# A streaming encoder layer on one core: the first part's stores on ScalarE's and GpSimd's queues, v loads asked for later, a buffer for the bias constant, and transposes held back

## The chip, the cores and the metric

The kernel runs on one core of a Trainium2 chip. It has a matrix engine (TensorE, PE in the profile), a vector engine (VectorE, DVE), a scalar engine (ScalarE, ACT), a general engine (GpSimd, POOL) and a queue engine that only issues transfers (SyncE, SP). Each engine works off its own instructions in their order and waits on semaphores for the others. Transfers between the on-chip memory and HBM are issued from SP, ACT or POOL and are carried out by 16 DMA engines. The metric is the device time of one execution in microseconds.

## What is computed

One layer of an encoder over 2048 prompt rows and 64 sample rows of width 1024. A conditioned norm is followed by one combined projection; its columns go to a gated convolution of width 31 (with layer norm and swish), to attention over the own chunk of 64 rows and the eight chunks before it (with a norm of q and k and a learned bias by distance), and to two gates. The two mixers are merged and projected; then comes a conditioned norm and a gated feed-forward network.

```
h = rms_norm(x, norm1_g) * (1 + sc1) + sh1
z = h @ w_in
glu_a, glu_b, q, k, v, g_conv, g_attn = split(z)
u = glu_a * sigmoid(glu_b)
conv_out, conv_state = conv_module(u, conv_hist, ...)
q = rms_norm(q, q_norm_g); k = rms_norm(k, k_norm_g)
o = attend(q, k, v)            # band of 9 chunks, softmax
merged = sigmoid(g_conv) * conv_out + sigmoid(g_attn) * (o @ w_attn_out)
x = x + gt1 * (merged @ w_o)
h2 = rms_norm(x, norm2_g) * (1 + sc2) + sh2
gate, up = split(h2 @ w_ffn_in)
x = x + gt2 * ((silu(gate) * up) @ w_ffn_out)
```

The outputs are the new rows of both sequences, the last 30 rows of the convolution's input, and the k and v rows that are kept (the last 512 of the prompt, the 64 of the sample).

## The kernel before

**Precision.** Every fp32 product is three products of rounded halves: an operand is split into a high part (`hi`, a copy by ACT in the rounded type) and a low part (`lo`, source minus high, by DVE or POOL), and `mm3` adds high x high, high x low and low x high. So each intermediate that goes to HBM for a later product goes as two stores, `hi` and `lo`.

**Two parts.** The first part works through four blocks of about 512 rows (`PBLOCKS`) in the order of `ORDER`: for each block q, a quarter of the convolution's input, k, another quarter, v, two more quarters, then the 16 column groups of the gates. It leaves q, k, v, the attention output, the convolution output and the gates in HBM (`q_d`, `k_d`, `v_d`, `o_d`, `c_d`, `g_d`). The second part (`CBLOCKS`) merges, projects and runs the feed-forward network from there.

**How work is interleaved.** The Python code keeps a planner, `Stream`, with an estimated load per engine in ns. `stream.at(t, f)` puts off `f` until the planner's TensorE time has passed `t`; `stream.when("dve")` is the time by which DVE is expected to have done what it was given; generators in lanes (`work` for q and k rows, `attn`, `conv`, `tail`, `norm_lane`) yield the time from which they may go on. `PE_LAG` is 400 ns. The lane `work` holds at most three rows; starting a fourth pushes the oldest on. The framework below assigns buffers and semaphores and may issue an instruction ahead of ones written earlier when its operands and its buffer are free: the bias rows are written after the second quarter of the convolution, yet their first operation runs at 65.15 us.

**Weights.** `Weights.split` (L294) loads or splits a weight tile into `whi` and `wlo` (five buffers each). For keys used again (`in` and `qkv` in the first part, `fi` and `fo` in the second), `then` (L332) stores both halves on SP at L336, and later blocks load them at L313. For `in` and `qkv` the low half is made by DVE.

**Rows of q and k.** `qk_rows` (L825) squares and copies the row's PSUM bank on ACT, reduces on DVE, takes the inverse root on POOL (`r`), scales on DVE (`kn`), and after `PE_LAG` goes to `store_kq` (L794): four transposes on PE, `hi` on ACT, `lo` on DVE into a pair of buffers (`parts`, two of each), and two stores on SP (L810). Kept k rows go out at L844.

**Rows of v.** `store_v` (L814) writes a tile `vst`, of which there is one buffer; it is stored on SP at L821. Kept v rows go out at L854.

**Convolution states.** `convolve` (L1008) transposes 30 columns of `u` on PE as soon as it starts (first and last block) and stores them at L1017. `conv_norm` stores its halves at L1079, `finish_head` those of the attention at L1178.

**Attention.** `attend(i)` (L1216 on) fetches the head's q, k and v, computes scores and softmax, and then the product with v. `load_v` (L1151 on, transfers at L1154 and L1156) uses the tag `vv` with two buffers; the v of head i+1 is asked for at the beginning of head i, when its buffer is still that of head i-1.

**Bias.** `bias_rows` (L774) writes a table of 128 shifted copies of the bias by one 3 MB transfer on ACT's queue (L784, called the skew transfer), and then two copies of a constant from the tile `far` (L788) into the same table. `far` comes from the seven buffers of `temp`.

Of the kernel before, what the change touches and what calls it, by code (L numbers as in the profile page):

```python
# [16 lines left out]
P = 128  # L17
# [24 lines left out]
PL_LESS = 9e9  # L42
TT_LESS = 9e9
PE_LAG = 400.0
ON_ACT = (3,)
ON_POOL = ()
DMA_LAG = 4000.0
# [167 lines left out]
class Weights:  # L215
# [78 lines left out]
    def split(self):  # L294
        i = len(self.ready)
        key = self.keys[i]
        if key[0] == "mod":
            (src,), a, b = self.source(key)
            w = self.pool.tile([P, a, b], F32, tag="whi", name="wmod", bufs=self.held)
            self.sync.dma_start(w, src)  # L300
            self.ready.append((w, None))
            return
        its = self.need.get(i, ())
        if i in self.first:
            shape = [P, 4 * len(key) - 4, P]
        else:
            shape = list(self.loaded[its[0]].shape) if its else self.stored[key][1]
        hi = self.pool.tile(shape, F32R, tag="whi", name="whi", bufs=self.held)
        lo = self.pool.tile(shape, F32R, tag="wlo", name="wlo", bufs=self.held)
        self.ready.append((hi, lo))  # L310
        if not its:
            for t, d in zip((hi, lo), self.stored[key][0]):
                self.sync.dma_start(t.bitcast(F32), d)  # L313
            return
        e, name = (self.dve, "dve") if key[0] in ("in", "qkv", "fi") or key[0] == "wo" and key[1] % 2 else (self.gps, "pool")
        if i in self.first:
            parts = [(slice(4 * j, 4 * j + 4), self.operand(f, op)) for j, (f, op) in enumerate(key[1:])]
            self.stream.after("act", "pool")
        else:
            parts = [(slice(0, shape[1]), self.loaded[its[0]])]  # L320
        for c, src in parts:
            self.act.activation(hi[:, c], src, AF.Copy)
            self.stream.after(name, "act")
            e.tensor_tensor(lo[:, c], src, hi[:, c].bitcast(F32), ALU.subtract)
        n = 0
        for j in its:
            self.users[j] -= 1
            if not self.users[j]:
                self.loaded.pop(j)
                n = j + 1 + self.staging  # L330

        def then():  # L332
            if key in self.again and key not in self.stored:
                ds = [self.dram.tile(shape, F32, name="w_d" + "_".join(map(str, key)) + "_" + part) for part in "hl"]
                for t, d in zip((hi, lo), ds):
                    self.sync.dma_start(d, t.bitcast(F32))  # L336
                self.stored[key] = ds, shape
            self.load_to(n)

        self.stream.at(self.stream.when(name), then, True)  # L340
# [87 lines left out]
def streaming_layer(ctx: ExitStack, tc: tile.TileContext, I, O):  # L428
# [147 lines left out]
    def temp(name, shape=(P, 512)):  # L576
        return wk.tile(list(shape), F32, tag="t", name=name, bufs=NT)

    def parts(n=None, shape=(P, 512)):
        return (  # L580
            wk.tile(list(shape), F32R, tag="sh", name="part_h", bufs=NS),
            wk.tile(list(shape), F32R, tag="sl", name="part_l", bufs=NS),
        )
# [103 lines left out]
    def mod_steps():  # L687
        for c6, half in MOD_HALVES:
            pa = ps_g.tile([P, 512], F32, tag="gp", name="pa")
            mod_sums(pa[:, : 2 * P], [("mod", c6, half, i) for i in range(4)])  # L690
            R = mod_rows(pa[:, : 2 * P])
            stream.at(
                stream.when("dve"), lambda pa=pa, R=R, c6=c6, half=half: mod_columns(pa[:, 2 * P :], R, c6, 4 * half, 2)
            )
            yield
        stream.flush()
        pt = ps_g.tile([P, 512], F32, tag="gp", name="pt")
        pe.transpose(pt[:32, :P], gates_c.rearrange("p c s k -> p (c s k)"), ident)
# [75 lines left out]
    def bias_rows():  # L774
        rv = wk.tile([NH, 257], F32, tag="bias", name="rv", bufs=1)
        nc.scalar.dma_start(rv, I["rel_bias"].rearrange("l h r -> (l h) r"))
        rr = wk.tile([NH, 768], F32, tag="kk", name="rr", bufs=1)
        dve.memset(rr[:, :511], 0.0)
        dve.tensor_scalar(rr[:, :511], rr[:, :511], rv[:, 256:], 8.0, ALU.add, ALU.mult)
        dve.tensor_scalar(rr[:, 511:], rv[:, ::-1], 8.0, None, ALU.mult)  # L780
        nc.scalar.dma_start(rb_d, rr)

        skew = bass.AP(tensor=sk_d.tensor, offset=sk_d.offset, ap=[[(P + 1) * 768, NH], [769, P], [1, 768]])
        nc.scalar.dma_start(skew, rb_d.unsqueeze(1).to_broadcast([NH, P, 768]))  # L784
        far = temp("far")
        dve.memset(far, BIG)
        for r, c in ((0, 576), (HD, 0)):
            nc.scalar.dma_start(  # L788
                sk_d[:, r : r + HD, P - 1 + c : P - 1 + c + HD].rearrange("h q c -> q h c"),
                far[:HD].rearrange("p (h c) -> p h c", h=NH),  # L790
            )


    def store_kq(src, n, dst, col, g=None):  # L794

        pt = ps_g.tile([P, 4, P], F32, tag="gp", name="pt")
        for hp in range(4):
            pe.transpose(pt[:, hp, :n], src[:n, hp * P : (hp + 1) * P], ident[:n, :n])
        stream.after("act", "pe")
        hi, lo = parts(shape=(P, 4, P))  # L800
        if g is None:
            split(hi[:, :, :n], lo[:, :, :n], pt[:, :, :n])
        else:
            act.activation(hi[:, :, :n], pt[:, :, :n], AF.Copy, scale=g)
            stream.after("dve", "act")
            dve.scalar_tensor_tensor(lo[:, :, :n], pt[:, :, :n], g, hi[:, :, :n].bitcast(F32), ALU.mult, ALU.subtract)

        def store():
            for j, t in enumerate((hi, lo)):
                nc.sync.dma_start(dst[j, :, :, col : col + n].rearrange("h p t -> p h t"), t[:, :, :n].bitcast(F32))  # L810

        stream.at(stream.when("act", "dve"), store)

    def store_v(src, n, row):  # L814
        vst = wa.tile([P, 4, 4, HD], F32R, tag="vst", name="vst", bufs=1)
# [5 lines left out]
        stream.at(stream.when("act", "dve"), lambda: nc.sync.dma_start(  # L821
            v_d[row : row + n].rearrange("t h d -> t (h d)"), vst[:n].rearrange("p a c d -> p (a c d)").bitcast(F32)
        ))

    def qk_rows(ps, n, g, dst, col, out_rows):  # L825
# [14 lines left out]
        if out_rows is not None:  # L840
            ko = temp("ko", (P, NH, HD))
            e, name = either(512, TT_LESS)
            e.tensor_tensor(ko[:n], kn[:n], gk[:n].unsqueeze(1).to_broadcast([n, NH, HD]), ALU.mult)
            stream.at(stream.when(name), lambda: nc.sync.dma_start(out_rows, ko[:n].rearrange("p h d -> p (h d)")))  # L844
        yield t + PE_LAG
        store_kq(kn.rearrange("p h d -> p (h d)"), n, dst, col, g)

    def v_rows(ps, n, t):
        out = state_row(vs_p, vn_s, t, n)
        store_v(ps, n, kcol(t))  # L850
        if out is not None:
            v32 = temp("v32")
            act.activation(v32[:n], ps[:n], AF.Copy)
            stream.at(stream.when("act"), lambda: nc.sync.dma_start(out, v32[:n]))  # L854

    def cached_kv():
        rows_ = [(src, j) for j in range(CACHE // P) for src in (ck, cv)]
# [150 lines left out]
    def convolve(u, y, ct, b):  # L1008
        w = UW if b == 0 else HIST + QB
        n = w - HIST  # L1010
        states = [(cs_s, HIST + SMP)] if b == 0 else [(cs_p, w)] if b == len(PBLOCKS) - 1 else []
        for rows_, e in states:
            pt = ps_g.tile([P, 512], F32, tag="gp", name="pt")
            pe.transpose(pt[:HIST, :P], u[:, e - HIST : e], ident)
            s = wa.tile([HIST, P], F32, tag="cc", name="cc", bufs=2)
            dve.tensor_scalar(s, pt[:HIST, :P], 0.5, None, ALU.mult)
            stream.at(stream.when("dve"), lambda s=s, rows_=rows_: nc.sync.dma_start(rows_[:, ct * P : (ct + 1) * P], s))  # L1017
            yield
        gps.tensor_copy(hist[:, ct], u[:, w - HIST : w])
        dve.tensor_scalar(y[:, ct, :n], u[:, :n], wd[:, ct, 0:1], bdw[:, ct : ct + 1], ALU.mult, ALU.add)  # L1020
# [4 lines left out]
    def conv_norm(y, c0, n, t0):  # L1025
# [38 lines left out]
        for ct in range(4):  # L1064
# [9 lines left out]
            yield stream.when("act")  # L1074
            name = low(hi[:, :n], lo[:, :n], tmp[:, :n], n, TT_LESS)

            def store(ct=ct, hi=hi, lo=lo):
                for l, a in enumerate((hi, lo)):
                    nc.sync.dma_start(c_d[l, ct, :, t0 : t0 + n], a[:, :n].bitcast(F32))  # L1079

            stream.at(stream.when(name), store)

    def gates(b, free):

# [76 lines left out]
    def finish_head(h, po, n, q0, key):  # L1161
# [10 lines left out]
        if i:  # L1172
            yield stream.when("dve")
            hi, lo = parts()
            split(hi[:, :n], lo[:, :n], o32[:, :n])
            def store():
                for l, a in enumerate((hi, lo)):
                    nc.sync.dma_start(o_d[l, h // 2, :, q0 : q0 + n], a[:, :n].bitcast(F32))  # L1178

            stream.at(stream.when("dve"), store)  # L1180

    def spans(b):

# [32 lines left out]
    def attend(i):  # L1216
# [4 lines left out]
        fetch_v(i)  # L1221
        yield loaded[i]
        (q2, kk), (_, bias), vnow = now["qk", i], now["bias"], now["v", i]
        fetch_v(i + 1)
        tiles = []
        for t in range(0, nq, P):
            n = min(P, nq - t)
# [556 lines left out]
```

## Time and profile before

| | us |
|---|---|
| median of 3 runs | 3119.94 |
| lowest, highest | 3117.39, 3123.71 |
| the profiled execution | 3121.02 |
| its span | 3119.2 |

Of the span TensorE is busy 2973.2 us (95%), VectorE 1782.7 (57%), ScalarE 1179.4 (38%) and GpSimd 1020.0 (33%). 657.09 MB go through SP's hardware queue, 20.76 MB through ScalarE's.

In the rows below, a time is in us from the span's start; "out<-in" names what is written and read; L97 is the helper through which every compute instruction is issued, so groups are told apart by their tiles; SPq, ACTq and POOLq are the queues that issue transfers. In brackets stands the idle time of the engine before an instruction, and what ended it. PE's clock is a share of its full rate.

### The profile page before, as it was taken

To read this page: it belongs to the slowest core of one execution; us is meant where nothing else is said; L and a number is where in the kernel's file an instruction comes from. 1 tells how busy PE (TensorE), PEld (TensorE's weight loads), DVE (VectorE), ACT (ScalarE), POOL (GpSimd) and SP (SyncE) were. 2 spreads that over 40 slices of the span, in tenths; PEclk is the share of its full clock that TensorE was granted. 3 is DMA by queue.
4 is the path that set the end of the run, shared out by engine and by line. 5 is a ranking of instruction groups with operands and counts; after the bars stand their busy time and mean duration, and the time that the engine had idled before them with its cause. 6 is when DMAs were issued, how large, how long until landed. Compare 5 with 4: busy or idle time off the path is not lost. (4 is left out here: it accounts for less than half of the span.)

```text
span 3119.2 us, 44388 instructions
## 1 busy us (share of the span) xinstructions
PE 2973.2 (95%) x16403; PEld 2641.3 (85%) x16403; DVE 1782.7 (57%) x3437; ACT 1179.4 (38%) x2105; POOL 1020.0 (33%) x638
## 2 busy tenths in 40 slices
PE   7799989998999999998999999999999999999999
PEld 4689867887788788798888898889999988999998
DVE  5598777776877895454433335454444555344344
ACT  3234531452254257355333342453333244332321
POOL 1100210111011102328666773434445342343331
PEclk9899999999999999999999999999999999999999
DMA  8799888887887788776444459655444975434434
GB/s 294 252 306 306 260 267 292 268 268 245 269 281 255 248 277 265 245 240 219 153 170 149 159 181 328 216 195 166 151 150 138 319 227 191 127 114 133 135 115 159
DMA packets 481814, 680.71 MB, mean 218 GB/s; under 512 B 38373, under 2 KB 316729, under 8 KB 481598
## 3 DMA queue, kind: packets, MB, share of 16 engines
q1 hardware_dynamic: 467157, 657.09, 64.2%
q10 hardware_dynamic: 14248, 20.76, 1.9%
q8 instruction: 129, 2.11, 0.3%
q14 instruction: 88, 0.71, 0.1%
q0 software_dynamic: 192, 0.04, 0.0%
HBM read 505.89 MB, written 175.01 MB: 218 GB/s over the span
## 5 line engine op out<-in xcount | busy, mean ns | idle before, releaser
L97 POOL TENSOR_TENSOR wlo<-wst,whi 128x1024 fp32r<-128x1024 f32 (+1 forms) x296 | 642.9, 2182 | 825.0 <-ACT whi L97 729.6
L97 ACT ACTIVATE whi<-wst 128x1024 fp32r<-128x1024 f32 (+1 forms) x361 | 354.0, 987 | 577.8 <-PE pd L97 234.0
L97 PE MATMUL ps<-t,whi 128*128 128x352 f32 (+2 forms) x2112 | 510.5, 326 | 23.7 <-ACT u L97 14.7
L97 PE MATMUL pd<-whi,hid 128*128 128x512 f32 (+1 forms) x1496 | 466.6, 390 | 0.1
L97 PEld LDWEIGHTS ps<-t,whi 128*128 128x128 f32 x2112 | 370.8, 190 | 30.0 <-ACT u L97 17.0
L97 PE MATMUL ps<-b,whi 128*128 128x352 f32 (+2 forms) x1584 | 387.4, 327 | 7.1 <-ACT early L97 5.8
L97 PE MATMUL ps<-hh,whi 128*128 128x512 f32 (+2 forms) x992 | 366.7, 370 | 9.9 <-DMA whi<-w_din_h 4.8
L97 DVE SCALAR_TENSOR_TENSOR y<-u,wd,y 128x512 f32<-128x512 f32 (+1 forms) x480 | 369.1, 773 | 7.4
L97 PE MATMUL ps<-hh,wlo 128*128 128x512 f32 (+2 forms) x992 | 348.5, 351 | 0.3 <-DMA wlo<-w_din_l 0.3
L97 PE MATMUL ps<-hl,whi 128*128 128x512 f32 (+2 forms) x992 | 348.5, 351 | 0.0
L97 PE MATMUL ps<-t,wlo 128*128 128x352 f32 (+2 forms) x1056 | 342.9, 325 | 0.0
L97 PEld LDWEIGHTS pd<-whi,hid 128*128 128x128 f32 (+1 forms) x1496 | 276.3, 185 | 62.9 <-issue 0.5
L97 DVE TENSOR_TENSOR acc<-acc,pd 128x512 f32<-128x512 f32 (+1 forms) x272 | 186.9, 687 | 201.6 <-PE pd L97 201.6
L97 PE MATMUL pd<-wlo,hid 128*128 128x512 f32 (+1 forms) x748 | 291.9, 390 | 0.7 <-DMA wlo<-w_dfo_l 0.7
L97 PEld LDWEIGHTS ps<-b,whi 128*128 128x128 f32 x1584 | 278.4, 190 | 11.3 <-ACT early L97 7.8
L97 PE MATMUL ps<-b,wlo 128*128 128x352 f32 (+2 forms) x792 | 257.3, 325 | 0.0
L97 POOL TENSOR_TENSOR r<-t,mhalf 128x1 f32<-128x1 f32 (+3 forms) x68 | 82.6, 1218 | 468.4 <-DVE t L97 468.1
L97 PEld LDWEIGHTS ps<-hh,whi 128*128 128x128 f32 x992 | 190.3, 192 | 28.6 <-DMA whi<-w_din_h 5.2
L97 PEld LDWEIGHTS ps<-hh,wlo 128*128 128x128 f32 x992 | 189.5, 191 | 23.4 <-DMA wlo<-w_din_l 0.6
L97 PEld LDWEIGHTS ps<-hl,whi 128*128 128x128 f32 x992 | 190.4, 192 | 15.8 <-issue 1.7
L97 PEld LDWEIGHTS ps<-t,wlo 128*128 128x128 f32 x1056 | 200.3, 190 | 0.0
L97 PE MATMUL ps<-cin,whi 128*128 128x384 f32 (+2 forms) x768 | 185.5, 328 | 7.0 <-DVE t L97 4.5
(198 smaller groups left out, 5106.4 us busy)
## 6 DMA issues: line engine op xcount, KB each, us to landing
wst<-sum_d SPq DMA_DIRECT2D x176, 256.0 KB, 2.7
whi<-w_din_h SPq DMA_DIRECT2D x72, 512.0 KB, 6.8
wlo<-w_din_l SPq DMA_DIRECT2D x72, 512.0 KB, 6.9
wst<-in_w_ffn_in SPq DMA_DIRECT2D x112, 256.0 KB, 3.1
wst<-in_w_ffn_in SPq DMA_DIRECT2D x49, 512.0 KB, 4.2
wmod<-in_w_ada SPq DMA_DIRECT2D x48, 512.0 KB, 7.0
wst<-in_w_o SPq DMA_DIRECT2D x48, 512.0 KB, 4.9
sum_d<-ws SPq DMA_DIRECT2D x88, 256.0 KB, 2.0
```

The lines of the kernel that those rows point to most:

```text
L97: return f(*args, **kw)
```

## The change

- High halves of `in` and `qkv` weights, of q, k, the convolution and the attention are stored from ACT's queue, low halves from POOL's. The helper `store_parts` issues the high half at once and the low half when DVE is expected to be done.
- v tiles, kept k rows and the convolution states are stored from POOL's queue, kept v rows from ACT's.
- `far` takes a buffer of the tag `vv`, in place of one of `temp`'s.
- The v of head i+1 is asked for when head i-1 has finished.
- `TURN_LAG` = 2500 ns takes the place of `PE_LAG` before the transposes of q and k rows, and is put ahead of those of the convolution states and of the modulation's column products.

```diff
+TURN_LAG = 2500.0
@@ split
+        on_dve = key[0] in ("in", "qkv")
@@ then
-                for t, d in zip((hi, lo), ds):
-                    self.sync.dma_start(d, t.bitcast(F32))
+                queues = (self.act.engine, self.gps.engine) if on_dve else (self.sync, self.sync)
+                for q, t, d in zip(queues, (hi, lo), ds):
+                    q.dma_start(d, t.bitcast(F32))
@@
+    def store_parts(dst, hi, lo, name="dve"):
+
+        nc.scalar.dma_start(dst[0], hi.bitcast(F32))
+        stream.at(stream.when(name), lambda: nc.gpsimd.dma_start(dst[1], lo.bitcast(F32)))
@@ mod_steps
-                stream.when("dve"), lambda pa=pa, R=R, c6=c6, half=half: mod_columns(pa[:, 2 * P :], R, c6, 4 * half, 2)
+                stream.when("dve") + TURN_LAG, lambda pa=pa, R=R, c6=c6, half=half: mod_columns(pa[:, 2 * P :], R, c6, 4 * half, 2)
@@ bias_rows
-        far = temp("far")
+        far = wk.tile([P, 512], F32, tag="vv", name="far", bufs=2)
@@ store_kq
-        def store():
-            for j, t in enumerate((hi, lo)):
-                nc.sync.dma_start(dst[j, :, :, col : col + n].rearrange("h p t -> p h t"), t[:, :, :n].bitcast(F32))
-
-        stream.at(stream.when("act", "dve"), store)
+        store_parts([dst[j, :, :, col : col + n].rearrange("h p t -> p h t") for j in range(2)], hi[:, :, :n], lo[:, :, :n])
@@ store_v
-        stream.at(stream.when("act", "dve"), lambda: nc.sync.dma_start(
+        stream.at(stream.when("act", "dve"), lambda: nc.gpsimd.dma_start(
@@ qk_rows
-            stream.at(stream.when(name), lambda: nc.sync.dma_start(out_rows, ko[:n].rearrange("p h d -> p (h d)")))
-        yield t + PE_LAG
+            stream.at(stream.when(name), lambda: nc.gpsimd.dma_start(out_rows, ko[:n].rearrange("p h d -> p (h d)")))
+        yield t + TURN_LAG
@@ v_rows
-            stream.at(stream.when("act"), lambda: nc.sync.dma_start(out, v32[:n]))
+            nc.scalar.dma_start(out, v32[:n])
@@ convolve
+        if states:
+            yield stream.when("dve") + TURN_LAG
...
-            stream.at(stream.when("dve"), lambda s=s, rows_=rows_: nc.sync.dma_start(rows_[:, ct * P : (ct + 1) * P], s))
+            stream.at(stream.when("dve"), lambda s=s, rows_=rows_: nc.gpsimd.dma_start(rows_[:, ct * P : (ct + 1) * P], s))
@@ conv_norm
-            stream.at(stream.when(name), store)
+            store_parts([c_d[l, ct, :, t0 : t0 + n] for l in range(2)], hi[:, :n], lo[:, :n], name)
@@ finish_head
-            stream.at(stream.when("dve"), store)
+            store_parts([o_d[l, h // 2, :, q0 : q0 + n] for l in range(2)], hi[:, :n], lo[:, :n])
@@ attend
-        fetch_v(i + 1)
...
         while now["finished"] < i - 1:
             yield lambda: now["finished"] == i - 1
+        fetch_v(i + 1)
```

More of the change, by code (lines that the diff above doesn't have):

```diff
@@ L1075, in conv_norm @@
             name = low(hi[:, :n], lo[:, :n], tmp[:, :n], n, TT_LESS)
-            def store(ct=ct, hi=hi, lo=lo):
-                for l, a in enumerate((hi, lo)):
-                    nc.sync.dma_start(c_d[l, ct, :, t0 : t0 + n], a[:, :n].bitcast(F32))
-            stream.at(stream.when(name), store)
+            store_parts([c_d[l, ct, :, t0 : t0 + n] for l in range(2)], hi[:, :n], lo[:, :n], name)
     def gates(b, free):
@@ L1175, in finish_head @@
             split(hi[:, :n], lo[:, :n], o32[:, :n])
-            def store():
-                for l, a in enumerate((hi, lo)):
-                    nc.sync.dma_start(o_d[l, h // 2, :, q0 : q0 + n], a[:, :n].bitcast(F32))
-            stream.at(stream.when("dve"), store)
+            store_parts([o_d[l, h // 2, :, q0 : q0 + n] for l in range(2)], hi[:, :n], lo[:, :n])
     def spans(b):
```

## The prediction

> **What bounds the kernel now.** I read the busy time by stage first. The columns are stretch, length, busy time and count of TensorE (PE), its weight loads, VectorE (DVE), ScalarE (ACT) and GpSimd (POOL), then the granted clock of PE, the DMA share and GB/s.
>
> ```profile
> 0.00:60.00 60.00, 43.19 (x266) 25.45 (x267) 27.22 (x73) 17.12 (x33) 9.58 (x20) 1.00 0.86 284
> 60.00:1255.00 1195.00, 1119.49 (x6265) 950.25 (x6265) 916.50 (x1890) 487.83 (x949) 148.78 (x134) 0.97 0.83 271
> 1255.00:3119.20 1864.20, 1810.55 (x9876) 1665.61 (x9874) 838.93 (x1474) 674.44 (x1123) 861.65 (x484) 0.99 0.55 182
> ```
>
> PE is the bound in all three. The change touches the first part only, up to about 1255 us. There PE is idle for 1195.00 - 1119.49 = 75.5 us between 60 and 1255; the 16.8 us before it are the start, and the 53.7 us behind it belong to stages whose code stays. So 75.5 us, plus what the clock loses around the stalls, is all that can be won. The table of PE's waits in that stretch says what ended them (total us, times, longest):
>
> ```profile
> PE pt L97 <- DVE kn L97: 20.2, 10, 4.8
> PE pt L97 <- ACT tb L97: 11.6, 1, 11.6
> PE sc L97 <- DMA kk<-k_d: 9.1, 6, 4.9
> PE ps L97 <- DMA whi<-w_dqkv_h: 6.5, 5, 3.1
> PE ps L97 <- DMA whi<-w_din_h: 4.8, 2, 3.9
> PE pa L97 <- DVE R L97: 4.6, 5, 1.3
> PE ps L97 <- DVE part_l L97: 4.5, 1, 4.5
> ```
>
> These seven rows are 61.3 of the 75.5 us. Next come the waits of SP's queue, which issues nearly all transfers in its order:
>
> ```profile
> SPq L1154 <- PE po L97: 79.3, 20, 10.8
> SPq L821 <- DVE vst L97: 54.6, 15, 9.0
> SPq L810 <- ACT part_h L97: 52.6, 16, 16.4
> SPq L313 <- DMA g_d<-gate: 13.7, 9, 5.5
> ```
>
> SP stands still for stores whose data aren't ready (L821, L810) and for a v buffer still being read (L1154); every load behind them waits too. The last row is a weight load that waits for a gate store with which it shares no buffer: transfers also wait for transfers issued before them, whichever queue issued those. One place in the timeline shows what that costs PE (start, length, what, idle before and its releaser):
>
> ```profile
> 412.38 1.22 SPq L1178 DMA_DIRECT2D o_d<-part_h  x1
> 415.08 0.60 SPq L1148 DMA_DIRECT2D kk<-k_d  x1
> 418.82 0.77 PE L97 MATMUL sc<-kk,q 128*64 128x320 f32 x2 [4.88 <-DMA kk<-k_d]
> 420.84 0.77 PE L97 MATMUL ps<-whi,hh 128*128 128x512 f32 x1 [1.25 <-DMA whi<-w_dqkv_h]
> ```
>
> A row of stores goes out up to 414, the key load only at 415.08, and PE stands for 4.88 us and again for 1.25. The stores are what the change takes out of this queue.
>
> A stall has a second price. Behind the wait of 4.5 us that ended just before 96 us, the granted clock is halved for some 3 us; in the middle of a busy stretch it is full:
>
> ```profile
> 96.00:99.00 3.00, 3.00 (x13) 3.00 (x14) 0.29 (x1) 0.00 (x0) 0.00 (x0) 0.51 0.14 54
> 117.00:130.00 13.00, 13.00 (x61) 10.30 (x60) 12.48 (x16) 2.25 (x4) 0.00 (x0) 1.00 1.05 355
> ```
>
> So a long stall costs about 3.0 x 0.49 = 1.5 us more than itself.
>
> **The change, part by part: what can be won.** The sum is made against the profiled run's own 3121.0 us (span 3119.2), which is 1.1 us above the shown median.
>
> *Row turns held back.* The planner puts the transposes of a q or k row 2500 ns behind its scaling instead of 400, so PE meets them up to 2.1 us later, with matmuls in between.
>
> ```profile
> 759.00 1.09 PE L97 MATMUL pt<-ident,kn 128*128 128x128 f32 x4 [4.76 <-DVE kn L97]
> ```
>
> This one would keep 4.76 - 2.1 = 2.7 us. Ten waits of 2.0 us on average could vanish but for such rests; against that, the lane that holds the rows admits three, and in the first block, where five rows end close together, it pushes the oldest out whatever its due time. I take half of the 20.2: **10 us**, bounds 4 and 18. The same delay for the conv-state transposes helps the next term, and for the modulation it touches the 4.6 us on R, which I leave out.
>
> *The stores of the first block around the skew transfer.*
>
> ```profile
> 74.65 0.76 ACTq L784 DMA_DIRECT2D sk_d<-rb_d  x1
> 90.45 0.69 ACT L97 ACTIVATE part_h<-pt,gqk 128x512 fp32r<-128x512 f32 x1 [6.20 <-DMA q_d<-part_h]
> 113.92 0.39 PE L97 MATMUL pt<-ident,u 128*30 128x128 f32 x1 [11.63 <-ACT tb L97]
> L788 ACTq DMA_DIRECT2D sk_d<-far x2: 657/825/993, 155.2 to 155.9; - x2
> ```
>
> The 3 MB skew transfer goes out on ACT's queue at 74.65; q stores issued just behind it on SP's queue hold their buffers until 90.45 and later, ACT waits for the buffers, the tanh behind it is late, and PE stalls for 4.5 and 11.6 us. Afterwards the high halves leave on ACT, right behind the skew, and the two copies of the bias constant (L788) can move up behind it too, since their source no longer waits for a shared buffer; they write into what the skew writes, so ACT would wait for it in order. That makes the first stall longer, at worst by the 6.20 us of that wait once more; I take 1.6, a quarter. But low halves no longer queue behind high ones, so the second stall, where SP fed one pair at a time, should shrink from 11.6 to about 3. Of 16.1 that leaves 4.5 + 1.6 + 3 = 9.1, a win of **7 us**, bounds -6 and 16.
>
> *Loads no longer behind stores, and v asked for later.* Key loads: 9.1 us in six waits, of which the one shown is half. I take **5**, bounds 2 and 9. Weight loads: 11.3 us, but some of it is no store's doing:
>
> ```profile
> 807.08 3.91 SPq L313 DMA_DIRECT2D whi<-w_din_h  x2
> 815.42 0.80 PE L97 MATMUL ps<-hh,whi 128*128 128x512 f32 x1 [3.87 <-DMA whi<-w_din_h]
> ```
>
> Here the modulation has just used up its weight buffers and the load can't go earlier. I take **2**, bounds 0 and 11.3 - 3.9 = 7.4. The v load is issued once the head before has ended; a v tile is wanted only behind the scores and softmax of its own head, so the 79.3 us of SP's waits go and nothing new waits. Without that cover a load would cost PE its landing, at least the 3.0 us that a store of its size takes below.
>
> *Clock.* Three long stalls gone or cut short (113.92, 418.82, 759.00) give 3 x 1.5 = **4.5 us**, bounds 0 and 9 (six).
>
> Won: 10 + 7 + 5 + 2 + 4.5 = 28.5 us, between 0 and 59.4.
>
> **What it costs.** From the code, 117 stores go to ACT (36 high halves of weights, 36 of q and k, 20 of conv, 20 of attention, 5 v rows) and 144 to POOL (the same 112 low halves, 19 v tiles, 5 k rows, 8 conv states).
>
> ```profile
> L1093 ACTq DMA_DIRECT2D g_d<-gate x84: 326/326/390, 230.9 to 1250.5; - x84
> L594 POOL DMA_DIRECT2D r<-in_norm_g x2: 536/645/754, 1.3 to 2.4; - x2
> L594 POOL DMA_DIRECT2D r<-in_b_ada x1: 549/549/549, 4.5 to 4.5; - x1
> r<-in_b_ada POOLq DMA_DIRECT2D x1, 24.0 KB, 6.1
> v_d<-vst SPq DMA_DIRECT2D x18, 512.0 KB, 3.0
> ```
>
> ACT issues a store in 326 ns: 117 x 0.326 = 38 us beside 487.83 us of work in 1195. Behind such an issue stand the tanh and the splits that free PSUM banks for PE; with ACT busy 41% I take **2 us**, bounds 0 and 38. POOL issues in about 0.55 us, and six times the rows (8 against 48) cost nothing that shows: 144 x 0.55 = 79 us beside 148.78, so POOL stays under a fifth. Behind its stores stand the row norms (r), whose lateness the held-back turns cover; that is 0 on top of the first term.
>
> A store from POOL lands late: 6.1 us for 24 KB against 3.0 for SP's 512 KB. This matters most where one buffer turns, the v tile:
>
> ```profile
> 486.57 0.60 ACT L97 ACTIVATE vst<-ps 128x512 fp32r<-128x512 f32 x1 [5.83 <-PE ps L97]
> 488.30 0.33 SPq L821 DMA_DIRECT2D v_d<-vst  x1
> 491.45 0.60 ACT L97 ACTIVATE vst<-ps 128x512 fp32r<-128x512 f32 x1 [4.29 <-DMA v_d<-vst]
> ```
>
> The waits on this ring so far, on ACT and on PE:
>
> ```profile
> ACT vst L97 <- DMA v_d<-vst: 47.1, 11, 8.0
> PE ps L97 <- DVE vst L97: 0.6, 1, 0.6
> ```
>
> A turn takes 491.45 - 486.57 = 4.9 us, and PE makes a v row in 24 matmuls of 13.00 / 61 = 0.213 us, 5.1 us: the ring just keeps up. With 3.1 us more landing and 0.2 more issue it takes 8.2, and each further row of a block falls 3.1 us behind: 13 such rows (4 + 3 + 3 + 3), 40 us of lateness on ACT. A block ends some 9 to 12 us late, which holds two or three of the five PSUM banks; PE runs on with the others. I take **4 us**, one per block, bounds 0 and 40. The loads of q, k and v at a block's start wait for the last stores, 4 x 3.1 = 12 us; five weight buffers ahead hide most: **2 us**, bounds 0 and 12.
>
> Descriptors written by GpSimd share a port with VectorE, and the trace shows such a pair blocking: the same POOL operation takes 0.55 us alone and 2.34 beside VectorE's scaling of x.
>
> ```profile
> 9.44 0.55 POOL L97 TENSOR_TENSOR r<-t,mhalf 128x1 f32<-128x1 f32 x1 [1.52 <-DVE t L97]
> 10.79 2.07 DVE L97 TENSOR_SCALAR x_t<-x_t,r 64x1024 f32<-64x1024 f32 x3
> 10.94 2.34 POOL L97 TENSOR_TENSOR r<-t,mhalf 128x1 f32<-128x1 f32 x1 [0.95 <-DVE t L97]
> ```
>
> The Trainium skill, SBUF — State Buffer, section "Who interferes with whom", has this as an exclusive lock that also keeps GpSimd from writing descriptors, and advises against GpSimd for stores next to VectorE; no run here shows it for a store. By that rule each of 144 stores may wait as long as the pair above did, which would feed the slower rival below.
>
> Cost 2 + 4 + 2 = 8. Net 28.5 - 8 = 20.5 us: 3121.0 - 20.5 = **3100**, 0.66% less.
>
> **The rivals.** *A, nothing to speak of:* the DMA engines are 83% busy in the stretch and the bytes stay the same; loads that pass the stores land later because the stores move beside them, and the stalls only change place. For it: the weight waits behind the modulation. Against it: at 412 to 421 us the load was late by its issue, not its transfer. Wins of 2 to 14 us, half of what I sum at best, against 8 of cost: 3115 to 3127, say 3121. The Trainium skill, DMA: Bandwidth & Descriptors, section "Issuing engines are not separate DMA queues", speaks for it: transfers from any issuer interleave on the same engines, and another issuer saves only issue time. SP's waits above show a saving that this sentence doesn't count, the standing behind unready stores.
>
> *B, slower:* the v ring becomes the limit. ACT issues in order; while it waits for the single v buffer, the tanh and splits behind it wait, banks aren't freed and PE stands for the whole lateness: 3121.0 - 28.5 + 2 + 2 + 40 = 3136.5. It decides once more than 24.5 of the 40 us reach PE, that is under 16 us of cover in four blocks. For it: the ring has no slack now. Against it: PE waited only 0.6 us on this ring so far, with 47.1 us of ACT's waits in it (the last two rows).
>
> *C, much faster:* all upper bounds of the wins together, 3121.0 - 59.4 + 8 = 3070. Against it: the first block's forced rows and the modulation's weights.
>
> **How the numbers follow.** Forecast 0.56, with 3080 to 3112 as its own range; A 0.12; B 0.26; C 0.06. The range runs from below C's 3070 to B with the skew term at its middle, 3136.5 + 5: 3066 to 3142. A measurement of this kernel tells about 0.2%, 6.2 us: the forecast and C lie below that (0.62), A within it (0.12), B above (0.26).
>
> **What would show it.** Right: PE idle between 60 and 1255 falls from 75.5 to about 50; PE's waits on kn fall to about 10 us and on kk to about 4; the 11.6 us wait on tb is gone or a few us, with a longer one at 91 to 99; SP's waits at the stores and at L1154 are gone; the stretch behind the first part keeps its 1864 us. Wrong: ACT waits on the v store well over 47 us in total with PE waits on vst or on PSUM banks behind them (B); or POOL issues of over 2 us, with r and kn late again.

## The result and the profile after

| | before | after |
|---|---|---|
| median, us | 3121.82 (4 runs) | 3150.63 (4 runs) |
| lowest to highest | 3117.39 to 3123.71 | 3143.79 to 3155.97 |
| ratio, 95% interval | | 1.0088 (1.0067 to 1.0109) |
| span of the profiled execution | 3119.2 | 3153.8 |

The change made the kernel 0.9% slower (the medians alone give 1.0092, inside the interval). The profiled execution is the slowest of the four after the change, so the spans differ by more, 34.6 us. Nearly the whole of it lies in the first part. The first matmul of the second part, that of the tile `cin`, starts at 1252.3 before and at 1285.4 after (rows of that tile in a window around this time: count, shortest, median and longest ns, first and last start):

```profile
L97 PE MATMUL ps<-cin,whi x190: 307/310/633, 1252.3 to 1339.8; 128*128 128x320 f32 x128, 128*128 128x384 f32 x62
```

```profile
L98 PE MATMUL ps<-cin,whi x128: 308/308/632, 1285.4 to 1321.6; 128*128 128x320 f32 x128
```

That is 33.1 us of the 34.6 by which the spans differ. The same two stretches by busy time, before and then after, in the columns of the prediction's first fence:

```profile
60.00:1252.30 1192.30, 1116.79 (x6248) 947.55 (x6247) 915.21 (x1888) 486.70 (x948) 148.62 (x134) 0.97 0.83 271
```

```profile
60.00:1285.00 1225.00, 1127.50 (x6249) 955.82 (x6248) 909.06 (x1886) 489.49 (x947) 233.76 (x272) 0.97 0.80 263
1285.00:3153.80 1868.80, 1819.02 (x9892) 1674.66 (x9892) 842.99 (x1477) 676.03 (x1125) 863.25 (x486) 0.99 0.55 182
```

PE's idle time rose from 75.5 to 97.5 us. Another 10.7 us are PE itself: one matmul more takes 1127.50 instead of 1116.79 us, and the mean granted clock of the span went from 0.984 to 0.978. DVE did the same work in 6 us less. What ended PE's waits after the change, from 60 to 1285 us (`sc` are scores, `pt` and `ptp` transposes, `kk` the keys, `kn` the normed q and k rows, `sm` and `pr` steps of the softmax):

```profile
PE pt L98 <- DVE kn L98: 19.4, 5, 13.6
PE sc L98 <- DVE sm L98: 14.3, 8, 4.2
PE ptp L98 <- DVE pr L98: 12.9, 7, 8.2
PE sc L98 <- DMA kk<-k_d: 12.1, 7, 3.2
PE ps L98 <- DMA whi<-w_dqkv_h: 9.6, 3, 4.7
PE ps L98 <- DMA whi<-w_din_h: 7.8, 4, 3.8
...
PE pa L98 <- DVE R L98: 1.2, 2, 0.6
```

The wait of 11.6 us on tb and that of 4.5 us on part_l are gone. The waits on kn are half as many but nearly as long in sum (19.4 us against 20.2), and those on softmax steps (sm, pr) and on loads grew. SP's queue in the same stretch:

```profile
SPq L314 <- PE ps L98: 266.0, 53, 23.1
SPq L270 <- DVE wlo L98: 96.2, 17, 15.0
SPq L1156 <- PE po L98: 90.2, 23, 9.9
...
SPq L1156 <- DMA v_d<-vst: 32.7, 4, 9.4
```

SP no longer stands at stores. It stands at loads instead: weight loads whose buffers PE still reads (L314; 109.8 us before), raw weights whose staging buffers aren't split yet (L270), and the v load (L1156), for which it waits no less than the 79.3 us before. The last row is the v load waiting until the stored v tiles have landed, once per block; before the change it was

```profile
SPq L1154 <- DMA v_d<-vst: 12.4, 4, 5.6
```

Where in the first part the time goes is seen from the carry of the convolution's last columns (POOL, `hist<-u`), which each quarter of each block does once. The fourth and the fifth of them, before and after:

```profile
228.68 3.08 POOL L97 COPY hist<-u 128x30 f32<-128x30 f32 x1 [16.45 <-DVE u L97]
...
410.28 0.39 POOL L97 COPY hist<-u 128x30 f32<-128x30 f32 x1 [10.03 <-DVE sm L97]
```

```profile
227.81 0.20 POOL L98 COPY hist<-u 128x30 f32<-128x30 f32 x1 [2.25 <-DVE u L98]
...
430.36 0.21 POOL L98 COPY hist<-u 128x30 f32<-128x30 f32 x1 [1.26 <-DVE u L98]
```

At 228 us the two kernels stand level. By 430 the changed one is 20 us behind, some 60% of the whole loss, and the last 13 come in small pieces up to the end of the part.

### The profile page after: what moved, and what is told of

The parts are those of the page before. It is cut to its first block, busy times and chain, and to the rows that moved or that the text cites. A ratio compares the mean times of both kernels' runs of the same rounds, so it can differ in the third digit from the quotient of the medians.

```text
span 3153.8 us, 44495 instructions
## 1 busy us (share of the span) xinstructions
PE 2989.1 (95%) x16403; PEld 2655.9 (84%) x16403; DVE 1781.0 (56%) x3437; ACT 1183.0 (38%) x2105; POOL 1109.1 (35%) x782
## 5 line engine op out<-in xcount | busy, mean ns | idle before, releaser
L98 PE MATMUL ps<-t,whi 128*128 128x352 f32 (+2 forms) x2112 | 513.1, 327 | 21.7 <-ACT u L98 14.1
L98 PEld LDWEIGHTS ps<-hl,whi 128*128 128x128 f32 x992 | 192.3, 194 | 16.1 <-issue 1.7
L98 ACT ACTIVATE pr<-pr,sm 128x640 f32<-128x640 f32 (+5 forms) x168 | 127.3, 764 | 159.7 <-DVE sm L98 157.9
```

Source lines behind the costliest of these rows:

```text
L98: return f(*args, **kw)
```

## The experiments

All ratios are to the kernel before, measured on the same chip, with 95% intervals in brackets.

**One part at a time.** The first four kernels take the change apart.

```
s_only_stores  before + all edits of stores, nothing else
s_only_turns   before + TURN_LAG = 2500.0 in its three places
s_only_v       before + fetch_v(i + 1) moved behind the wait for "finished"
s_no_stores    before + turns, v, and far in the tag "vv" (the change without its stores)
```

> Before, with the stores of the first part on ScalarE's and GpSimd's queues and nothing else changed. Theory R (the routing costs: a low half issued by GpSimd lands 6.2 us after its issue instead of 3.2 to 3.6, the ring of two part buffers turns later, VectorE and ScalarE wait in order): ratio to before 1.008 to 1.013, the first part ends 25 to 40 us later than before, low halves of q and k land in about 6 us. Theory T (the held-back turns or the later v load cost, the routing is harmless): ratio 0.993 to 1.002. Theory O (only the mixture costs, by another order of the work): within 0.998 to 1.004.

> Before, with the turns of the q and k rows, the modulation rows and the conv states held back by 2500 ns and nothing else. Theory R: the ten waits of PE on kn (20.2 us) fall by about half and the ratio is 0.994 to 0.999. Theory T: the softmax and score steps behind a held-back turn come late, ratio 1.005 to 1.011. Theory O: within 0.998 to 1.003.

> Before, with the v load of the next head asked for once the head before has ended, and nothing else. Theory R: nothing new waits on PE; SP's wait for PE's po at the v load (79.3 us) stays, as it did in the changed kernel (90.2 us), since the old request only waited in the same place; ratio 0.998 to 1.001. Theory T: v lands late, PE waits on v for 3 us a head, ratio 1.003 to 1.008. Theory O: 0.998 to 1.002.

> The changed kernel with its stores back on SP's queue (turns held back, v asked for later, bias constant in its own buffer). Theory R: the loss goes with the routing, ratio to before 0.993 to 1.000. Theory T: the loss stays, ratio 1.006 to 1.011. Theory O: somewhere between, 0.999 to 1.005, and not the sum of the single parts.

| kernel | ratio |
|---|---|
| stores alone | 1.0124 (1.0104 to 1.0144) |
| turns alone | 0.9999 (0.9984 to 1.0013) |
| v alone | 0.9987 (0.9972 to 1.0001) |
| turns, v and the bias constant, no stores | 0.9994 (0.9978 to 1.0009) |

The stores carry the loss, all of it. The other parts are worth nothing that can be measured. (With the v load alone moved, SP's waits for PE at it fell from 79.3 to 51.6 us, and nothing came of it.) Beside the routed stores they may take something back (1.0088 for the whole change against 1.0124), two intervals that just touch, and no run separates this further; the bias constant wasn't run alone. With the turns alone, PE's waits (60 to 1255 us) show why ten waits on kn were worth so little:

```profile
PE pt L98 <- DVE kn L98: 16.1, 4, 7.9
PE ps L98 <- DVE part_l L98: 11.4, 1, 11.4
```

Six of ten waits vanish, but the four that are left are longer, 16.1 us against 20.2, and the wait on part_l in the first block grows from 4.5 to 11.4.

**Which stores, and which queue.** Theory P (GpSimd is the cost) against theory A (ScalarE is), and the weights against the rest. The stores that an edit doesn't name stay on SP.

```
s_hi_act       high halves and kept v rows on ACT (117 stores)
s_lo_pool      low halves, v, kept k rows, conv states on POOL (144 stores)
s_only_wst     weight halves: high on ACT, low on POOL (72 stores)
s_only_parts   q, k, conv and attention halves: high on ACT, low on POOL
s_all_act      every one of the 261 stores on ACT
s_ring3        s_only_stores with three low-half buffers:
-        wk.tile(list(shape), F32R, tag="sl", name="part_l", bufs=NS),
+        wk.tile(list(shape), F32R, tag="sl", name="part_l", bufs=3),
-    NT, NS = 7, 2
+    NT, NS = 6, 2
s_ring3_sp     before with the same two edits
```

> Before, with only the high halves (117 stores) issued on ScalarE's queue; low halves, v, k rows and conv states stay on SP's. Theory P (GpSimd's part costs: late landing, and its in-order waits for VectorE's low halves hold up the row norms): ratio 0.996 to 1.003, and PE's waits on kn stay near 20 us. Theory A (ScalarE's in-order issues cost): ratio 1.006 to 1.013, with ScalarE late for PE's banks.

> Before, with only the low halves, v, k rows and conv states (144 stores) issued on GpSimd's queue; high halves stay on SP's. Theory P: ratio 1.008 to 1.013, POOL waits of 300 us and more for VectorE at its stores, low halves landing in 6 us, DVE and POOL steps behind them late. Theory A: ratio 0.998 to 1.004.

> Before, with only the 72 weight stores routed (36 on ScalarE, 36 on GpSimd). Theory P1 (the weight halves are the cost: a weight's low half holds its buffer longer, the staging load behind it is late, PE waits on whi): ratio 1.005 to 1.012. Theory P2 (the two-buffer ring of the q, k, conv and attention parts is the cost, the weights are not): ratio 0.998 to 1.003.

> Before, with all 261 stores of the first part on ScalarE's queue, none on GpSimd's and none on SP's. Theory P (GpSimd's issues land late, and its stores wait in order ahead of its own work): ratio 0.996 to 1.004, since no store lands late. Theory S (SP's queue without stores runs ahead into weight loads whose buffers PE still reads, and the q, k and v loads stand behind those): ratio 1.006 to 1.012, with SP's waits for PE at the weight loads well over 200 us as in the routed kernel, against 110 before.

> The routed stores of the first run with a third buffer for the low halves (paid for by one of the seven temporaries). Theory P: VectorE no longer waits for the landing of a low half; the loss of 1.24% falls to 0.3 to 0.7%. Theory S: the loss stays, 1.010 to 1.015.

> The control for the third buffer: before, with three low-half buffers and six temporaries, stores on SP. Both theories: ratio 0.998 to 1.004.

> Before, with only the halves of q, k, conv and attention routed (72 high on ScalarE, 76 low on GpSimd); weights, v, k rows and conv states stay on SP. Theory P: 1.005 to 1.010, most of the loss, since here the ring of two buffers turns. Theory S: 1.002 to 1.006, since weight and v stores still pace SP's queue.

(By the prediction's counts the routed halves of that last kernel are 76 and 76, not 72 and 76.)

| kernel | stores off SP | ratio |
|---|---|---|
| high halves on ACT | 117 | 0.9987 (0.9977 to 0.9997) |
| q, k, conv, attention halves | 152 | 1.0002 (0.9989 to 1.0015) |
| weight halves | 72 | 1.0030 (1.0017 to 1.0042) |
| low halves, v and rows on POOL | 144 | 1.0068 (1.0054 to 1.0081) |
| all, three low buffers | 261 | 1.0106 (1.0085 to 1.0127) |
| all on ACT and POOL | 261 | 1.0124 (1.0104 to 1.0144) |
| all on ACT | 261 | 1.0135 (1.0114 to 1.0156) |
| three low buffers, stores on SP | 0 | 1.0008 (0.9992 to 1.0024) |

Three of these lie where neither theory had put them: 1.0068, 1.0135, and 1.0002 for the halves that turn the ring.

The pair of high and low halves (0.9987 against 1.0068) spoke for theory P. The kernel with nothing on POOL at all spoke against it: with every store on ACT the loss is as large, so GpSimd isn't needed for it. In the whole change POOL's stores do land later. The page's list of transfers (count, KB, median us from issue to landing) has for the whole change:

```profile
k_d<-part_l POOLq DMA_DIRECT2D x18, 256.0 KB, 6.4
q_d<-part_l POOLq DMA_DIRECT2D x16, 256.0 KB, 6.2
```

and with all stores on ACT:

```profile
k_d<-part_l ACTq DMA_DIRECT2D x18, 256.0 KB, 5.2
q_d<-part_l ACTq DMA_DIRECT2D x16, 256.0 KB, 4.8
```

against 3.2 and 3.6 us on SP's queue before. (The queue alone doesn't set this: with the turns held back and every store on SP, the same rows say 5.4 and 5.6 us.) But a third buffer, which would take the lateness off DVE, changes 1.0124 to 1.0106 with overlapping intervals, and the 152 stores that turn this ring cost nothing as long as the other 109 stay on SP. The parts don't add: 117 stores on ACT are free, 144 on POOL cost 0.7%, and both together cost 1.2%. It isn't the number either: 152 routed stores are free, 72 cost 0.3%. What the losing kernels of this table share is that the low halves of the weights have left SP. Those that lose 0.7% or more share another thing: the v tiles have left SP too. No run moved either of the two alone, so the table doesn't say which of them costs.

**The order of the work.** The built programs show that the framework puts SP's loads into another order once the stores are gone: 161 of the 478 places of the first part differ between the kernel before and the one with routed stores, though the text asks for the loads in the same order (one expectation below says 121 of the first 470; the two orders written into the kernels differ there in 161). So theory S (this order costs) was tried against theory N (it doesn't matter) and theory Q (PE's own order costs), first by holding an engine to the order of the text:

```
+    held = ExitStack()
+    held.enter_context(tc.manual_schedule(engines={nc.sync.engine}))   # or nc.tensor.engine
     xs = first_rows()
...
+    held.close()
     side.close()
     p1.close()
```

> The routed stores of the first run, with SP's queue held to the order in which the kernel's text asks for its transfers, in the first part alone (the framework may no longer move a load ahead of another). Theory S (without the stores the framework moves weight loads ahead of q, k and v loads on SP, and these stand behind buffers still being read): most of the loss of 1.24% goes, ratio 0.998 to 1.005. Theory N (any routing off SP costs, whatever the order of the loads): 1.009 to 1.014.

> The control: before, with SP's queue held to the order of the text in the first part. Theory S: 0.997 to 1.004, few loads are moved before (40 overtakings against 89 with the stores routed). Theory N: the same, no claim.

> The routed stores with PE held to the order of the text in the first part, all else left to the framework. Theory Q (the routing costs because the framework orders PE's own matmuls worse when stores leave SP): ratio to the next kernel, before with the same hold, within 0.998 to 1.003. Theory S: the gap of 1.0 to 1.3% between the two stays, since SP's loads are still moved.

> The control: before, with PE held to the order of the text in the first part. All theories: slower than before by 0 to 1%, since PE can no longer fill a wait with other work that the framework sees.

| held to the text's order | stores routed | stores on SP |
|---|---|---|
| SP | 1.0288 (1.0270 to 1.0306) | 1.0313 (1.0294 to 1.0331) |
| PE | 1.0364 (1.0345 to 1.0383) | 1.0295 (1.0278 to 1.0312) |

None of the four came near its expected range: the text's order costs some 3% on either engine, so the framework's moving of instructions is worth that much to this kernel. With SP held, the routed stores lose nothing against the unrouted ones; with PE held they lose 0.7%. A loss of 1% could hide in a kernel that is 3% slower, so the orders that the framework itself had made were exchanged: each of the 478 loads chained behind the one that preceded it in the other kernel.

```
+    behind = mybir.DependencyInfo(mybir.DependencyClass.NoSync, mybir.DependencyReason.DATA)
+    for i, j in zip(SP_ORDER, SP_ORDER[1:]):
+        tc.add_manual_dep(loads[j], loads[i].name, behind, reason="SP_ORDER")
     side.close()
     p1.close()
```

> The routed stores of the first run, with SP's 478 loads of the first part held to the very order that the framework had given them before. Theory S (the order of SP's loads is the cost): the loss of 1.24% goes for the most part, ratio 0.998 to 1.005. Theory N (it is not, the stores cost wherever they are issued but on SP): 1.009 to 1.014.

> The reverse: before, its stores on SP, with SP's 478 loads held to the order that the framework gave them once the stores were routed (121 of the first 470 places differ). Theory S: it takes over the loss, ratio 1.006 to 1.014. Theory N: 0.998 to 1.003.

| | stores on SP | stores routed |
|---|---|---|
| loads in the order of before | 1 | 1.0130 (1.0106 to 1.0154) |
| loads in the order of the routed kernel | 1.0056 (1.0036 to 1.0077) | 1.0124 (1.0104 to 1.0144) |

Theory S falls as the main cause. The order alone costs 0.56%, between the two expected ranges, but the routing costs 1.3% with the old order too. Only the loads were pinned: the other engines' instructions were still the framework's to move, and an experiment that held all engines to the orders of before wasn't tried.

**Together.** The parts that were not above 1 alone:

```
s_hi_act_v     s_hi_act + fetch_v moved + far in the tag "vv"
```

> The parts that measured below 1 alone, together: high halves on ScalarE's queue, v asked for later, the bias constant in its own buffer; low halves stay on SP, turns as before. If the gains of 0.13% each add: 0.996 to 0.999. If the order of the loads moves again: anywhere from 0.994 to 1.006.

1.0001 (0.9987 to 1.0015). The gains of single parts don't add. The only kernel with its whole interval below 1 is the one with the high halves on ACT, 0.9987, 4 us; since this one, which contains it, stands at 1.0001, and 18 kernels were tried, that gain isn't firm.

## Where the time goes

The stretch from 200 to 260 us, where the raw weights still arrive and the attention of the first block begins, separates most of the slow kernels from the others. Its rows for the kernel before, for the halves of q, k, conv and attention routed, for all stores on ACT, and for all routed with the loads in the order of before:

```profile
200.00:260.00 60.00, 56.82 (x412) 55.68 (x411) 57.10 (x120) 24.99 (x54) 6.00 (x6) 0.97 0.89 299
```

```profile
200.00:260.00 60.00, 60.00 (x436) 58.83 (x436) 57.26 (x119) 25.14 (x56) 6.32 (x7) 0.97 0.87 291
```

```profile
200.00:260.00 60.00, 51.20 (x346) 48.93 (x345) 47.77 (x106) 19.71 (x45) 2.82 (x4) 0.91 0.80 270
```

```profile
200.00:260.00 60.00, 49.22 (x329) 48.04 (x330) 47.97 (x107) 19.02 (x45) 5.87 (x12) 0.89 0.76 261
```

Before, PE and DVE are both busy 95% of these 60 us and the DMA engines 89%, so there is little room in it to make up a loss. In the two slow kernels both engines work 5 to 9 us less, the clock is lower, and the DMA share falls. The splits of the raw weights by DVE (`wlo<-wst`: first and last start) end that much later, before and with all stores routed:

```profile
L97 DVE TENSOR_TENSOR wlo<-wst,whi x35: 1204/1218/1227, 42.3 to 321.7; 128x1024 fp32r<-128x1024 f32 x35
```

```profile
L97 DVE TENSOR_TENSOR wlo<-wst,whi x35: 1205/1221/1227, 40.8 to 338.9; 128x1024 fp32r<-128x1024 f32 x35
```

| kernel | ratio | PE busy, 200 to 260 | DVE busy | PE waits on kk, 205 to 265 | last split | SP waits until v has landed, 60 to 1300 |
|---|---|---|---|---|---|---|
| high halves on ACT | 0.9987 | 53.23 | 54.20 | 2.2 | 326.0 | 14.1 |
| before | 1 | 56.82 | 57.10 | 0 | 321.7 | 12.4 |
| q, k, conv, attention halves | 1.0002 | 60.00 | 57.26 | 0 | 320.7 | 14.6 |
| weight halves | 1.0030 | 52.65 | 50.07 | 5.9 | 329.9 | 19.6 |
| before, loads in the routed order | 1.0056 | 57.17 | 54.85 | 0 | 319.1 | 11.7 |
| low halves, v and rows on POOL | 1.0068 | 50.47 | 52.01 | 4.3 | 331.9 | 28.9 |
| the change | 1.0088 | 48.40 | 49.33 | 6.3 | 333.5 | 32.7 |
| all on ACT and POOL | 1.0124 | 49.62 | 50.13 | 5.9 | 338.9 | 34.6 |
| the same, loads in the order of before | 1.0130 | 49.22 | 47.97 | 7.4 | 341.3 | 32.7 |
| all on ACT | 1.0135 | 51.20 | 47.77 | 6.8 | 343.6 | 25.1 |

With one exception the ratios above 1.002 follow the last split, and with the same exception every kernel above 1.002 waits longer for v to land (last column) than those below. The busy times follow less well: the kernel with the high halves on ACT works 3 us less in the stretch and loses nothing. From 1.0068 up the lag at the last split, 10 to 22 us, is some half of the loss; the rest comes behind it. The exception, the kernel before with the loads in the routed order, loses later: over the first part PE waits 16.4 us on kk and 14.0 on w_dqkv, against 9.1 and 6.5 before. How the stretch goes wrong is seen in the kernel with all stores routed (timeline: start, length, what, idle before and its releaser; rows of SP's queue, then PE, ACT and DVE):

```profile
202.32 0.37 SPq L269 DMA_DIRECT2D wst<-in_w_in  x1
...
214.29 0.61 SPq L1146 DMA_DIRECT2D q<-q_d  x1
216.84 0.45 SPq L1147 DMA_DIRECT2D kk<-k_d  x1
...
223.22 0.50 PE L97 MATMUL sc<-kk,q 128*64 128x320 f32 x1 [5.91 <-DMA kk<-k_d]
...
231.28 1.06 ACT L97 ACTIVATE whi<-wst 128x1024 fp32r<-128x1024 f32 x1 [1.49 <-PE ps L97]
232.38 1.22 DVE L97 TENSOR_TENSOR wlo<-wst,whi 128x1024 fp32r<-128x1024 f32 x1 [0.48 <-ACT whi L97]
...
233.63 0.37 SPq L269 DMA_DIRECT2D wst<-in_w_in  x1
```

and in the kernel before:

```profile
221.12 0.61 SPq L1148 DMA_DIRECT2D kk<-k_d  x1
...
229.31 1.21 DVE L97 TENSOR_TENSOR wlo<-wst,whi 128x1024 fp32r<-128x1024 f32 x1
...
229.78 0.46 PE L97 MATMUL sc<-kk,q 128*64 128x320 f32 x2
```

Routed, the first half of the key load goes out at 216.84, 4.3 us *earlier* than before, and yet PE stands for it: the score matmul stands in PE's order where PE reaches it at 223.22 - 5.91 = 217.3 us, with the load just issued (its second half at 218.25). Before, PE comes to it only at 229.78, after weight matmuls. PE's stall holds the weight buffers, so ACT's next split waits for PE (231.28), DVE's follows it, and the next raw weight is asked for at 233.63. The split before this one was at 214.68, 17.7 us earlier; in the kernel before, the splits between 202 and 230 us follow each other in 5 to 8 us.

Between the first two of SP's rows above lies a second thing. SP came to the load of v and stood there for a v tile that was stored from POOL's queue at 200.70 and landed 10.8 us after its issue. Its waits from 200 to 225 us, with all stores routed, before, and routed with the loads in the order of before:

```profile
SPq L1153 <- DMA v_d<-vst: 8.8, 1, 8.8
```

```profile
SPq L1154 <- DMA v_d<-vst: 1.4, 1, 1.4
```

```profile
SPq L470 <- DMA v_d<-vst: 12.1, 1, 12.1
```

Behind it stood a raw weight, whose staging buffer DVE's split at 208.21 had freed by 209.4 and which went out at 213.68, and the keys. These have one buffer, which PE's scores at 212.23 read until 212.9, so the q load at 214.29 is at most 1.4 us late by the wait for v: here it explains little of PE's 5.9 us. Nor does it go with the loss everywhere. With every store on ACT, SP asks for the keys ahead of v in this stretch and doesn't wait for v there; with the weight halves alone routed it waits 9.9 us for v, and the kernel loses 0.3%. What the waits for v cost over the four blocks isn't shown, since no kernel was run with all stores routed but the v tiles.

So the trace's reading is that the framework, which sees SP free of stores, takes the keys to be there sooner and puts their matmuls ahead of the weights, in a stretch that can't spare 6 us. That is a reading of the traces and not shown by a run: with PE held to the text's order, 0.7% of the loss stays, in a kernel with other stalls. Open are which stores do it (the weights' low halves or the v tiles), and the last 13 us of the loss. Nor is every loss of the first block kept: the kernel with the halves of q, k, conv and attention routed has its fifth carry at 418.5 us, 8 us behind the kernel before, and ends the first part level with it.

## Why the prediction was wrong

The forecast was 3100 with a range of 3066 to 3142; the time is 3150.6, outside it. By its steps:

- *Row turns, 10 us.* The waits on kn went from ten to five (four with the turns alone), but the time didn't: the turns alone are worth 0.01%, within 0.15%. PE meets the remaining rows later and then waits longer, and another wait of the first block grew by 6.9 us.
- *The skew pair, 7 us.* Both of PE's waits went altogether, where 9.1 us of them were expected to stay. In their place came a wait of 13.6 us on kn that ended at 131.6, and ACT stood still while issuing (last section). At 228 us the kernels are level: 0 won, inside the bounds of -6 and 16.
- *Key loads 5, weight loads 2.* The waits grew instead, 9.1 to 12.1 and 11.3 to 17.4 us. That SP's waits for PE at the v load would go was wrong too: 79.3 became 90.2, and the v edit alone left the time within its error.
- *Clock, 4.5 us.* It went the other way: PE's own time grew by 10.7 us and the mean granted clock fell. PE's idle time grew too, by 22 us; that the stalls brought the clock down isn't shown apart.
- *ACT's issues, cost 2; POOL's, 0.* Right in sum: 117 stores on ACT cost nothing, and POOL issues in 543 to 785 ns on average. That every store on ACT takes 326 ns was not: one q store took 9.39 us (last section).
- *The v ring, 4 us, and rival B.* ACT's wait on the v store went from 47.1 to 50.3 us, with no wait of PE behind it; from POOL the tiles landed in 4.0 us (median), not 6.1.
- *The loads at a block's start, 2 us, bounds 0 and 12.* Mis-sized: SP's waits for v to land grew from 12.4 to 32.7 us, 20.3 more. How much of it reached PE no run shows.
- *The rivals.* Rival B had the nearest time (3136.5) for a reason that isn't there. The Trainium skill, SBUF — State Buffer, section "Who interferes with whom", stood beside it: by that lock POOL's issues would have taken up to 2.34 us each, and they took 0.83 at most.

The step that failed is "Loads no longer behind stores" (wins of 5 and 2 us, where the waits on keys and weights grew by 3.0 and 6.1), and with it the whole way of the sum. It took PE's waits from the trace of before, assigned each to a store, and let them shrink one by one with every other instruction in its place. What the runs showed in its place: the stores alone cost 1.24%. The loads did not run free; SP stood longer at weight buffers that PE still read (266.0 us against 109.8) and at v tiles that hadn't landed (32.7 against 12.4). And the instructions did not keep their places: 161 of SP's 478 loads moved, and in the stretch around 217 us PE's matmuls too, so the waits of before weren't there any more to be shortened, and others were. The order of the loads alone costs 0.56% and isn't the main cause; what the rest is made of stays open: PE's order and the landing of the v tiles are the two candidates that the traces show, and no run parts them. The prediction had read one row for the stretch from 60 to 1255 us, in which PE has 75.5 us of slack and DVE is busy 77%. Cut into stages, it would have shown 200 to 260 us with PE and DVE at 95% and the DMA engines at 89%, where the losing kernels fall 8 to 22 us behind by the last split.

What the Trainium skill says in DMA: Bandwidth & Descriptors, section "Issuing engines are not separate DMA queues", that another issuer saves only the time of issuing, stood behind rival A, and it fits what was won: nothing, or 0.13% for the high halves.

## What to carry to other kernels

Where a framework orders the instructions, moving transfers to another queue is not a local edit: compare the order of the two built programs before pricing a wait, and try the parts one by one, because their gains and losses don't add. Price an edit stage by stage and look first for the stage in which several engines are full at once; a loss there is hard to make up. Ask of each store which load needs its data: while it hasn't landed, that load stands in its queue, and everything behind it. And a queue that stands still at stores isn't always wasting the time: here the loads that came earlier stood as long at buffers that weren't free.

## What the runs showed of the hardware

Issuing a transfer can stop an engine. With all stores routed, ACT issues the 3 MB skew transfer at 92.06 and a q store behind it at 92.91; that issue alone takes 10.16 us (the median of these stores' 17 issues on ACT is 0.38), and ACT's next operation waits for it:

```profile
92.06 0.76 ACTq L791 DMA_DIRECT2D sk_d<-rb_d  x1
92.91 10.16 ACTq L583 DMA_DIRECT2D q_d<-part_h  x1
103.20 0.69 ACT L97 ACTIVATE part_h<-pt,gqk 128x512 fp32r<-128x512 f32 x1 [10.46 <-issue]
```

The whole change shows the same, 9.39 us at 95.21, and so does the kernel with only the high halves on ACT, 7.41 us at 98.30, which loses nothing by it. The issuing queue needn't be the one that holds the large transfer: in the kernel before, where the skew transfer goes out on ACT's queue at 74.65, SP's issue of a q store at 102.21 takes 5.15 us. What holds these issues up no run shows.

How late a store lands isn't a property of its queue alone. The medians for 256 KB low halves of q and k were 3.2 to 3.6 us on SP's queue in the kernel before but 5.2 to 5.7 on the same queue with the change's other parts and no routed store, 4.8 to 5.2 on ACT's with all stores there, and 6.2 to 6.4 on GpSimd's in the whole change.
